# The chunk scan of an S5 layer: step innermost in the state tile, state copies in stages, and a new order of the phase behind it

## The chip, the core and the metric

The kernel runs on one core of a Trainium2 chip. The metric is the device time of one execution in microseconds, as the median of three runs. Matrix products run on TensorE, elementwise work on VectorE (DVE) and ScalarE (ACT), a few memsets on GpSimd (POOL); transfers are queued on SyncE (SP) and on ScalarE's queue. All arithmetic is float32; the large products are made of three products of rounded halves (`hi*hi + hi*lo + lo*hi`).

## What is computed

The model is an encoder of two layers over 512 tokens of width 1024. Layer 0 mixes tokens with a bidirectional diagonal state-space model (S5) and a GLU, layer 1 with a short gated convolution; each layer then attends to 256 memory tokens and applies a squared-ReLU MLP. The change lies in layer 0's mixer:

```python
u = (h @ w_in).reshape(bsz, seq, SSM_GROUPS, SSM_GROUP)      # 64 groups of 16
y = d * u
for r in range(2):                                           # two directions
    a_bar = exp(lam * dt)                                    # complex, 64 states a group
    bu = einsum('gph,lbgh->lbgp', b_bar, u)                  # flipped in time for r == 1
    states = associative_scan(a_r * a_l, a_r * b_l + b_r)    # x[l] = a_bar * x[l-1] + bu[l]
    y = y + einsum('ghp,lbgp->blgh', c, states).real         # flipped back for r == 1
z = gelu(y)
z = z * sigmoid(z @ w_glu)
return z @ w_out
```

## The kernel before

The 512 tokens are cut into 64 chunks of 8 (`NC = 64`, `T = 8`). Within a chunk the recurrence is unrolled into matrices; from chunk to chunk a complex state per group and state index is carried. The partitions hold both directions: 0 to 63 forward, 64 to 127 backward.

The stages around the change are these.

- `s_mats` (line 523): TensorE forms each chunk's contribution to the state, and ScalarE copies it from PSUM into `estate`, a tile of 128 partitions x [64 steps, 2 parts (real, imaginary), 64 groups].
- `scan_ops` (line 595): for step s = 1 to 63, VectorE makes four instructions of 128 elements each: two multiplies of the previous state by the powers `a1` and `a2` into scratch, and two adds into `estate[:, s]`. All are issued through the helper `tt` (line 312). `scan_run(n)` (line 776) runs the next n steps; for the first 12, VectorE also builds the tables `Q` in between.
- `strips` and `y_intra` (lines 544 and 579): TensorE builds the within-chunk matrices and applies them. Between them `kvp(n)` (line 712) advances the generator `kv0_gen` (line 630), which computes keys and values of the first cross-attention as a filler: eight blocks of 16 matmul steps. When a block ends, ScalarE evacuates it, and the next block but one is loaded by a DMA from ScalarE's queue.
- `p_part` (line 661) copies states from `estate` into `pt`, one tile for each eighth of the groups, shifted by one step, and reversed in time for the backward half. `p_early` copies the steps 0 to 41 of the blocks 0 to 3 within the scan, on ScalarE; `p_copy` the rest behind the scan, forward on VectorE and backward on ScalarE. The slot that has no predecessor is set to zero in each `pt` by GpSimd.
- `y_carry(i)` (line 587): TensorE adds the carried states' part of the output of a quarter of the groups. `y_evac` copies it out of PSUM (ScalarE and VectorE one half each), `z_rows` transposes it on TensorE, `z_gelu` applies the gelu on ScalarE and splits the result into halves on VectorE.
- `lin_block` (line 170) is one block of a large linear layer: 8 k-steps of six matmuls. Its weights come as 1 MB blocks through two staging buffers (`pump_dma`), and are split into halves by ScalarE (line 143) and VectorE (line 144) in `pump_split`. The first GLU block, `glu0`, takes the last quarter's `z_rows` and `z_gelu` in a hook.

Up to `glu0` the instructions of each engine run in the order in which they are written (`tc.manual_schedule()`); from `man.close()` on a planner sets the order, and it may place later work (the casts of keys and values, lines 1002 to 1006) ahead. Small tiles come from a pool of 30 pages (`NPG`); `estate` shares one large buffer with the tiles before and after it. The order behind the scan is:

```python
    y_intra(3)
    p_copy(0)
    p_copy(1)
    act.activation(warm, epsb, AF.Gelu_apprx_tanh)
    y_carry(0)
    for b in range(2, 6):
        p_copy(b)
    yt = y_evac(0)
    y_carry(1)
```

Of the kernel before, what the change touches and what calls it, by code (L numbers as in the profile page):

```python
# [19 lines left out]
P = 128  # L20
S = 512
D = 1024
KT = D // P
# [23 lines left out]
def tile_encoder(ctx, tc, xT, xN, memT, memN, small, b_re, b_im, c_re, c_im, a_w_in, a_w_glu,  # L47
# [23 lines left out]
    def page(shape, dt=F32, name="pg"):  # L71
        return pgpool.tile([P] + list(shape), dt, tag="pg", name=nm(name))

    def bank(shape, name="ps"):
        return pspool.tile([P] + list(shape), F32, tag="ps", name=nm(name))
# [54 lines left out]
    def pump_dma(ahead):  # L130
        while pos["dma"] < len(stream) and pos["dma"] - pos["split"] < ahead:
            loaded.append(stage_load(stream[pos["dma"]]))
            pos["dma"] += 1

    def pump_split(ahead):
        while pos["split"] < pos["dma"] and pos["split"] - pos["use"] < ahead:
            st = loaded[pos["split"]]
            tiles = []
            for half in range(2):
                src = st[:, 4 * half:4 * half + 4, :]  # L140
                hi = page([4, 256], F32R, "wh")
                lo = page([4, 256], F32R, "wl")
                act.copy(hi, src)  # L143
                v.tensor_tensor(out=lo, in0=src, in1=hi, op=ALU.subtract)  # L144
                tiles.append((hi, lo))
            split.append(tiles)
            pos["split"] += 1
# [22 lines left out]
    def lin_block(xs, hooks=None):  # L170

        t = next_block()
        ps = [bank([S], "lin") for _ in range(2)]
        for k in range(KT):
            if hooks and k in hooks:
                for f in hooks[k]:
                    f()
            xh, xl = xs(k)
            for m in range(2):
                mm3(ps[m], wsl(t, k, m, 0), wsl(t, k, m, 1), xh, xl, k == 0, k == KT - 1)  # L180
        return ps
# [25 lines left out]
    def split_to(a, k, src, from_act=True):  # L207
        if from_act:
            act.copy(a.hi(k), src)
        else:  # L210
            v.tensor_copy(a.hi(k), src)
        v.tensor_tensor(out=a.lo(k), in0=src, in1=a.hi(k), op=ALU.subtract)
# [246 lines left out]

    bb = s5pool.tile([P, 2, 65 * 16], F32, name="bb")  # L460
    nc.gpsimd.memset(bb[:, :, 64 * 16:], 0.0)
    estate = bpool.tile([P, NC, 2, G], F32, tag="big", name="estate")

    def gen_ops(b, X, xs, E, E2, flip, name):

# [42 lines left out]
    def sf_transpose(b):  # L508
        outp = []
        for ri in range(2):  # L510
            pg = page([8, P], F32, "sf")
            for hb in range(2):
                ps = bank([4, P], "tr")
                for i in range(4):
                    g = 4 * hb + i
                    pe.transpose(ps[:, i, :], sfT[b][ri][:, g].rearrange("p h j -> p (h j)"), ident)  # L516
                act.copy(pg[:, 4 * hb:4 * hb + 4, :], ps)
            outp.append(pg)
        sf[b] = outp
# [2 lines left out]

    def s_mats(b):
        for ri in range(2):
            ps = bank([NC, 8], "ps_s")
            for g in range(8):
                u = U[b // 2][:, 8 * (b % 2) + g, :]
                for r in range(2):
                    rs = slice(64 * r, 64 * r + 64)
                    pe.matmul(ps[rs, :, g], lhsT=sf[b][ri][:, g, rs], rhs=u[:, ::-1] if r else u,  # L530
                              start=True, stop=True)
            act.copy(estate[:, :, ri, 8 * b:8 * b + 8], ps)

    Q = {}

# [51 lines left out]
    def y_carry(i):  # L587
        for g in range(8):
            for ri in range(2):
                for b2 in range(2):  # L590
                    pe.matmul(yps[i][g // 4][64 * b2:64 * b2 + 64, g % 4, :], lhsT=pts[2 * i + b2][:, ri, g, :],
                              rhs=Q[2 * i + b2][ri][:, g].rearrange("p t h -> p (t h)"),
                              start=False, stop=(ri == 1 and g % 4 == 3))

    def scan_ops():
        for s in range(1, NC):
            xp = estate[:, s - 1]
            x = estate[:, s]
            t1_ = s5pool.tile([P, 2, G], F32, tag="sc1", name=nm("sc1"))
            t2_ = s5pool.tile([P, 2, G], F32, tag="sc2", name=nm("sc2"))  # L600
            yield (t1_, xp, a1, ALU.mult)
            yield (t2_, xp[:, ::-1, :], a2, ALU.mult)
            yield (x, x, t1_, ALU.add)
            yield (x, x, t2_, ALU.add)
# [51 lines left out]
                kv_load(i + 2)  # L656
            yield

    SE = 42

    def p_part(b, s0, s1, engs):

        for ri in range(2):
            e = estate[:, s0:s1, ri, 8 * b:8 * b + 8].rearrange("p s g -> p g s")
            engs[0](pts[b][0:64, ri, :, s0 + 1:s1 + 1], e[0:64])
            lo, hi = NC - 1 - s1, NC - 1 - s0
            engs[1](pts[b][64:128, ri, :, lo:hi], e[64:128, :, ::-1])  # L667

    def p_tile(b):
        pt = page([2, 8, NC], F32, "pt")  # L670
        nc.gpsimd.memset(pt[0:64, :, :, 0:1], 0.0)
        nc.gpsimd.memset(pt[64:128, :, :, NC - 1:NC], 0.0)
        pts[b] = pt

    def p_early(b):
        p_tile(b)
        p_part(b, 0, SE, (act.copy, act.copy))

    def p_copy(b):
        if b in pts:  # L680
            p_part(b, SE, NC - 1, (v.tensor_copy, act.copy))
        else:
            p_tile(b)
            p_part(b, 0, NC - 1, (v.tensor_copy, act.copy))


    ups = {}
# [24 lines left out]
    def kvp(n):  # L712
        for _ in range(n):
            next(kv_it, None)
# [34 lines left out]
    sf_transpose(2)  # L749
    sf_step(5)  # L750
    sf_transpose(3)
    s_mats(0)
    s_mats(1)
    mem_scale(mp, rm, 0)
# [21 lines left out]
    def scan_run(n, extra=()):  # L776

        extra = list(extra)
        for i in range(n):
            for j in range(4):  # L780
                tt(*sc[ns[0]])
                ns[0] += 1
                if j >= 2 and extra:
                    tt(*extra.pop(0))
        run_ops(extra)
# [17 lines left out]
    kvp(16)  # L803
    y_intra(2)
    scan_run(20)
    kvp(16)
    for b in range(4):
        p_early(b)
    kvp(48)
    scan_run(63 - 43)  # L810


    zf = []
# [2 lines left out]
    def y_evac(i):  # L816
        yt = page([T, 8, 16], F32, "yt")
        for q in range(2):
            o = yt[:, :, 4 * q:4 * q + 4, :]
            src = yps[i][q].rearrange("p g (t h) -> p t g h", t=T)  # L820
            if q == 0:
                act.copy(o, src)
            else:
                v.tensor_copy(o, src)
        return yt
# [3 lines left out]
    def z_rows(i, yt):  # L829
        zps[i] = [bank([4, P], "zT") for _ in range(2)]  # L830
        for q in range(2):
            for t in range(4):
                pe.transpose(zps[i][q][:, t, :], yt[:, 4 * q + t].rearrange("p g h -> p (g h)"), ident)
# [9 lines left out]
            tt(z.l[i][:, :, c], zf[i][:, :, c], z.h[i][:, :, c], ALU.subtract)  # L843

    y_intra(3)
    p_copy(0)
    p_copy(1)
    act.activation(warm, epsb, AF.Gelu_apprx_tanh)
    y_carry(0)
    for b in range(2, 6):  # L850
        p_copy(b)
    yt = y_evac(0)
    y_carry(1)
    p_copy(6)
    p_copy(7)
    for i in range(1, 4):
        z_rows(i - 1, yt)
        yt = y_evac(i)
        if i < 3:
            y_carry(i + 1)  # L860
        z_gelu(i - 1)
        if i == 2:
            pump_dma(2)
            pump_split(1)
    glu0 = lin_block(z, {2: [lambda: z_rows(3, yt), lambda: z_gelu(3)]})
    pump_dma(2)
    man.close()
    s5.close()

    tpool = ctx.enter_context(tc.tile_pool(name="tpool", bufs=8, reuse_waits="tile"))  # L870
# [14 lines left out]
    def norm_feed(k, st, a, vec):  # L885
# [3 lines left out]
            stt(a.lo(k), hk(k), gain(vec, k), a.hi(k), ALU.mult, ALU.subtract)  # L889
        st.add(hk(k), k == 0)  # L890


    z2 = Act2("z2")
    for i in range(4):
        ps = lin_block(z) if i else glu0
        pump()
        for m in range(2):
            k = 2 * i + m
            sg = tmp("sg")
            act.activation(sg, ps[m], AF.Sigmoid)  # L900
            tt(sg, sg, zf[i][:, m, :], ALU.mult)
            split_to(z2, k, sg)

    def residual_linear(xs, vec, hooks=None):
        a = Act2("hn")
# [9 lines left out]

    hnA, st = residual_linear(z2, G_XATT)


    def kv_tiles():
        kv = bpool.tile([P, 4, 2048], F32R, tag="big", name=nm("kv"))  # L920
        kh = [kv[:, i, :].rearrange("p (k n) -> p k n", k=KT) for i in range(2)]
        vh = [kv[:, 2 + i, :].rearrange("p (m n) -> p m n", m=2) for i in range(2)]
        return kh, vh

    def attention(hn_, st, kh, vh, vec):
        qa = Act2("q")
# [69 lines left out]
        transposes(2)  # L996
        hooks = {2: [lambda: o_block(2)], 3: [lambda: transposes(3)], 5: [lambda: o_block(3)]}
        return residual_linear(oa, vec, hooks)

    kh, vh = kv_tiles()  # L1000
    for i in range(2):
        act.copy(kh[0][:, 4 * i:4 * i + 4, :], K0[i])
        tt(kh[1][:, 4 * i:4 * i + 4, :], K0[i], kh[0][:, 4 * i:4 * i + 4, :], ALU.subtract)
        c = slice(512 * i, 512 * i + 512)
        act.copy(vh[0][:, :, c], V0[i])
        tt(vh[1][:, :, c], V0[i], vh[0][:, :, c], ALU.subtract)

    hnF, st = attention(hnA, st, kh, vh, G_FFN)

# [231 lines left out]
```

## Time and profile before

| what | value |
|---|---|
| median of three runs | 1475.1 us (1473.31 to 1475.87) |
| the profiled execution's own time | 1473.65 us |
| its span in the trace | 1471.9 us |
| granted TensorE clock, mean | 0.992 |
| busy: TensorE, VectorE, ScalarE | 97%, 59%, 36% |
| HBM read, written | 148.08 MB, 6.16 MB |

The page lists the busy time of each engine, the span in 40 slices, the DMA queues, the chain of work that ended last, and the costliest groups of instructions. TensorE's share is an average: it is full in the linear layers, and less so in the state-space phase, up to about 220 us. That phase is read from three views: a table of windows (busy time of each engine in a stretch), the timeline (instructions in order of time, with the idle time ahead of them and what ended it), and the instructions grouped by line and shape. A group's mean is the duration of one instruction; the next one can start a little before it ends.

### The profile page before, as it was taken

How to read it: one execution, taken by the hardware profiler on the slowest of the kernel's cores; microseconds unless marked ns; L12 is line 12 of the kernel's file. 1: busy time of each engine (PE TensorE's matmuls, PEld its weight loads, DVE VectorE, ACT ScalarE, POOL GpSimd, SP SyncE). 2: the span in 40 equal slices, each digit the busy share in tenths (PEclk: the TensorE clock that was granted, in tenths of full speed). 3: DMA queues.
4: the chain of work that ended last, by engine and by line, in shares of the span. 5: the costliest groups of instructions: out<-in, count | busy, mean ns of one | idle time of the engine just before them, and what ended most of it. 6: DMA issues, size and time to landing. Idle time of an engine off the chain costs nothing.

```text
span 1471.9 us, 19469 instructions
## 1 busy us (share of the span) xinstructions
PE 1432.1 (97%) x8146; PEld 1178.2 (80%) x8146; DVE 865.9 (59%) x1377; ACT 534.0 (36%) x799; POOL 4.9 (0%) x25
## 2 busy tenths in 40 slices
PE   8998879999999999999999999999999999999997
PEld 3586667888888888888888888988888888888886
DVE  8999966556565444444457546556666444544435
ACT  4661364434444132232333324433444323132221
POOL 0000000000000000000000000000000000000000
PEclk9999989999999999999999999999999999999999
DMA  8616515222133323323123224523024323323201
GB/s 291 199 50 177 151 56 200 86 86 87 58 114 115 115 86 93 107 86 109 63 73 128 86 87 143 193 77 103 30 86 143 114 86 91 110 86 110 90 1 58
DMA packets 157304, 155.50 MB, mean 106 GB/s; under 512 B 11424, under 2 KB 152864, under 8 KB 157216
## 3 DMA queue, kind: packets, MB, share of 16 engines
q1 hardware_dynamic: 149888, 146.91, 31.7%
q10 hardware_dynamic: 7328, 7.34, 1.6%
q8 instruction: 64, 1.05, 0.3%
q14 instruction: 24, 0.20, 0.0%
HBM read 148.08 MB, written 6.16 MB: 105 GB/s over the span
## 4 chain that ended last, share of the span: by engine, by line
PE 92%; DVE 4%; ACT 2%; DMA 1%; issue 0%; SPq 0%; ACTq 0%; DVEq 0%
PE lin L166 26%; PE lin L168 26%; PE lin L167 26%; PE u L693 4%; DVE estate L312 1%; DVE sc L312 1%; PE kv L168 1%; PE kv L167 1%; PE kv L166 1%; ACT pt L667 1%; PE ps_s L530 1%; PE tr L516 1%; PE kv L641 1%; PE kv L639 1%; DMA wd<-wt 1%; DVE Q L312 1%
## 5 line engine op out<-in xcount | busy, mean ns | idle before, releaser
L144 DVE TENSOR_TENSOR wl<-st,wh 128x1024 fp32r<-128x1024 f32 x224 | 270.6, 1222 | 171.5 <-ACT wh L143 170.9
L143 ACT CAST wh<-st 128x1024 fp32r<-128x1024 f32 x224 | 231.5, 1049 | 320.6 <-PE lin L167 292.2
L166 PE MATMUL lin<-hnh,wh 128*128 128x512 f32 x832 | 326.0, 392 | 0.0
L168 PE MATMUL lin<-hnh,wl 128*128 128x512 f32 x832 | 323.7, 389 | 0.0
L167 PE MATMUL lin<-hnl,wh 128*128 128x512 f32 x832 | 323.7, 389 | 0.0
L166 PE MATMUL lin<-mid,wh 128*128 128x512 f32 (+1 forms) x528 | 202.4, 383 | 0.0
L168 PE MATMUL lin<-mid,wl 128*128 128x512 f32 (+1 forms) x528 | 202.0, 383 | 0.0
L167 PE MATMUL lin<-mid,wh 128*128 128x512 f32 (+1 forms) x528 | 202.0, 383 | 0.0
L167 PEld LDWEIGHTS lin<-hnl,wh 128*128 128x128 f32 x832 | 156.2, 188 | 33.4 <-issue 1.2
L166 PEld LDWEIGHTS lin<-hnh,wh 128*128 128x128 f32 x832 | 156.2, 188 | 33.3 <-issue 1.2
L168 PEld LDWEIGHTS lin<-hnh,wl 128*128 128x128 f32 x832 | 156.2, 188 | 32.6
L168 PEld LDWEIGHTS lin<-mid,wl 128*128 128x128 f32 x528 | 99.2, 188 | 19.4
L166 PEld LDWEIGHTS lin<-mid,wh 128*128 128x128 f32 x528 | 99.2, 188 | 19.4
L167 PEld LDWEIGHTS lin<-mid,wh 128*128 128x128 f32 x528 | 99.2, 188 | 19.3
L312 DVE TENSOR_TENSOR relu<-relu,lin 128x512 f32<-128x512 f32 x64 | 43.7, 683 | 104.6 <-ACT relu L1025 104.6
L312 DVE TENSOR_TENSOR mo<-lin,r 128x512 f32<-128x512 f32 (+1 forms) x66 | 44.2, 675 | 102.1 <-PE lin L168 101.9
L1025 ACT ACTIVATE relu<-lin 128x512 f32<-128x512 f32 x64 | 38.0, 594 | 128.4 <-PE lin L168 128.0
L888 ACT ACTIVATE hnh<-h,sm 128x512 fp32r<-128x512 f32 x40 | 28.7, 718 | 132.0 <-DVE h L312 118.8
L693 PE MATMUL u<-xbig,st 128*128 128x512 f32 x128 | 58.4, 616 | 6.3 <-DMA st<-in_a_w_in_dram 6.3
L312 DVE TENSOR_TENSOR h<-lin,h 128x512 f32<-128x512 f32 x32 | 21.8, 692 | 67.3 <-PE lin L168 57.8
L1027 ACT CAST mid<-relu 128x512 fp32r<-128x512 f32 x64 | 39.6, 618 | 42.5 <-DVE relu L312 41.8
L693 PEld LDWEIGHTS u<-xbig,st 128*128 128x128 f32 x128 | 25.1, 198 | 37.2 <-issue 30.3
(214 smaller groups left out, 1934.9 us busy)
## 6 DMA issues: line engine op xcount, KB each, us to landing
st<-in_f_w_dram SPq DMA_DIRECT2D x64, 1024.0 KB, 5.7
st<-in_b_w_in_dram SPq DMA_DIRECT2D x12, 1024.0 KB, 5.1
st<-in_x_w_kv_dram SPq DMA_DIRECT2D x10, 1024.0 KB, 5.3
st<-in_x_w_q_dram SPq DMA_DIRECT2D x8, 1024.0 KB, 5.2
st<-in_x_w_o_dram SPq DMA_DIRECT2D x8, 1024.0 KB, 5.2
st<-in_x_w_kv_dram ACTq DMA_DIRECT2D x6, 1024.0 KB, 7.3
mt<-wd SPq DMA_DIRECT2D x32, 128.0 KB, 3.8
st<-in_a_w_glu_dram SPq DMA_DIRECT2D x4, 1024.0 KB, 5.6
```

The lines of the kernel that those rows point to most:

```text
L143: act.copy(hi, src)
L144: v.tensor_tensor(out=lo, in0=src, in1=hi, op=ALU.subtract)
L166: pe.matmul(ps, lhsT=wh, rhs=xh, start=start, stop=False)
L167: pe.matmul(ps, lhsT=wh, rhs=xl, start=False, stop=False)
L168: pe.matmul(ps, lhsT=wl, rhs=xh, start=False, stop=stop)
L312: v.tensor_tensor(out=o, in0=a, in1=b, op=op)
L516: pe.transpose(ps[:, i, :], sfT[b][ri][:, g].rearrange("p h j -> p (h j)"), ident)
L530: pe.matmul(ps[rs, :, g], lhsT=sf[b][ri][:, g, rs], rhs=u[:, ::-1] if r else u, start=True, stop=True)
L693: pe.matmul(ups[i, m], lhsT=win[i][:, k, m * P:(m + 1) * P], rhs=hn[k // 2][:, k % 2, :], start=(k == 0), stop=(k == KT - 1))
L888: act.activation(a.hi(k), hk(k), AF.Copy, scale=gain(vec, k))
L1025: act.activation(r_, ps[m], AF.Relu)
L1027: act.copy(md[:, k, 0, :], r_)
```

## The change

- `estate` becomes 128 partitions x [2 parts, 64 groups, 64 slots]: the step is now innermost. Slot 0 is set to zero once, and the contribution of chunk c goes to slot c + 1, so that slot s holds the state that chunk s needs. The last chunk's contribution isn't kept. The scan runs over s = 2 to 63, 62 steps.
- `s_mats` writes its PSUM tile in the order [group, chunk].
- `p_part` copies both parts in one instruction, without a shift; all eight blocks are copied in three stages: slots 0 to 35 behind step 43 in the written order, 36 to 51 behind step 51 (both halves on ScalarE), 52 to 63 behind the scan (VectorE and ScalarE). The memsets of the `pt` tiles go.
- `kvp(16)` and `kvp(48)` become `kvp(20)` and `kvp(32)`, with the first stage of the copies between them.
- The gelu table's load moves ahead of the last 11 steps; `pump_dma(2)` ahead of the last stage of copies.
- Behind the scan, `y_carry(i)` stands ahead of `z_rows(i - 1)`, two weight blocks are split in the loop, and the hook of `glu0` moves from k = 2 to k = 4.
- The casts of keys and values move into the GLU blocks 2 and 3, and `man.close()` behind those blocks: they run in the written order too.

```diff
-    estate = bpool.tile([P, NC, 2, G], F32, tag="big", name="estate")
+    estate = bpool.tile([P, 2, G, NC], F32, tag="big", name="estate")
...
-            ps = bank([NC, 8], "ps_s")
+            ps = bank([8, NC], "ps_s")
...
-                    pe.matmul(ps[rs, :, g], lhsT=sf[b][ri][:, g, rs], rhs=u[:, ::-1] if r else u,
+                    pe.matmul(ps[rs, g, :], lhsT=sf[b][ri][:, g, rs], rhs=u[:, ::-1] if r else u,
...
-            act.copy(estate[:, :, ri, 8 * b:8 * b + 8], ps)
+            act.copy(estate[:, ri, 8 * b:8 * b + 8, 1:NC], ps[:, :, 0:NC - 1])
...
-        for s in range(1, NC):
-            xp = estate[:, s - 1]
-            x = estate[:, s]
+        for s in range(2, NC):
+            xp = estate[:, :, :, s - 1]
+            x = estate[:, :, :, s]
...
     def p_part(b, s0, s1, engs):
-        for ri in range(2):
-            e = estate[:, s0:s1, ri, 8 * b:8 * b + 8].rearrange("p s g -> p g s")
-            engs[0](pts[b][0:64, ri, :, s0 + 1:s1 + 1], e[0:64])
-            lo, hi = NC - 1 - s1, NC - 1 - s0
-            engs[1](pts[b][64:128, ri, :, lo:hi], e[64:128, :, ::-1])
...
+        if b not in pts:
+            pts[b] = page([2, 8, NC], F32, "pt")
+        e = estate[:, :, 8 * b:8 * b + 8, s0:s1]
+        engs[0](pts[b][0:64, :, :, s0:s1], e[0:64])
+        engs[1](pts[b][64:128, :, :, NC - s1:NC - s0], e[64:128][:, :, :, ::-1])
...
+    nc.gpsimd.memset(estate[:, :, :, 0:1], 0.0)
     s_mats(0)
...
     scan_run(20)
-    kvp(16)
-    for b in range(4):
-        p_early(b)
-    kvp(48)
-    scan_run(63 - 43)
+    kvp(20)
+    for b in range(8):
+        p_part(b, 0, 36, (act.copy, act.copy))
+    kvp(32)
+    scan_run(8)
+    for b in range(8):
+        p_part(b, 36, 52, (act.copy, act.copy))
+    act.activation(warm, epsb, AF.Gelu_apprx_tanh)
+    scan_run(62 - 51)
...
     y_intra(3)
-    p_copy(0)
-    p_copy(1)
-    act.activation(warm, epsb, AF.Gelu_apprx_tanh)
+    pump_dma(2)
+    for b in range(8):
+        p_part(b, 52, NC, (v.tensor_copy, act.copy))
     y_carry(0)
-    for b in range(2, 6):
-        p_copy(b)
     yt = y_evac(0)
-    y_carry(1)
-    p_copy(6)
-    p_copy(7)
     for i in range(1, 4):
+        y_carry(i)
         z_rows(i - 1, yt)
+        if i < 3:
+            pump_split(i)
         yt = y_evac(i)
-        if i < 3:
-            y_carry(i + 1)
         z_gelu(i - 1)
-        if i == 2:
-            pump_dma(2)
-            pump_split(1)
-    glu0 = lin_block(z, {2: [lambda: z_rows(3, yt), lambda: z_gelu(3)]})
+    glu0 = lin_block(z, {4: [lambda: z_rows(3, yt), lambda: z_gelu(3)]})
     pump_dma(2)
-    man.close()
     s5.close()
...
+    def kv_cast(i):
+        act.copy(kh[0][:, 4 * i:4 * i + 4, :], K0[i])
+        tt(kh[1][:, 4 * i:4 * i + 4, :], K0[i], kh[0][:, 4 * i:4 * i + 4, :], ALU.subtract)
+        c = slice(512 * i, 512 * i + 512)
+        act.copy(vh[0][:, :, c], V0[i])
+        tt(vh[1][:, :, c], V0[i], vh[0][:, :, c], ALU.subtract)
...
     for i in range(4):
         ps = lin_block(z) if i else glu0
         pump()
...
+        if i >= 2:
+            kv_cast(i - 2)
+    man.close()
```

## Rows read from the trace of the kernel before

**Rows 1.** Page, first part: busy us, share of the span, instructions, by engine.
```profile
PE 1432.1 (97%) x8146; PEld 1178.2 (80%) x8146; DVE 865.9 (59%) x1377; ACT 534.0 (36%) x799; POOL 4.9 (0%) x25
```

**Rows 2.** Table of windows: stretch, its length, busy us by engine, clock, DMA.
```profile
109.00:172.00 63.00, 56.43 (x832) 45.32 (x831) 60.94 (x184) 5.97 (x11) 1.44 (x12) 0.95 0.66 175
205.00:221.50 16.50, 11.65 (x177) 10.65 (x174) 9.32 (x14) 15.50 (x21) 0.00 (x0) 1.00 0.00 1
233.00:280.00 47.00, 47.00 (x209) 38.93 (x208) 23.63 (x29) 19.56 (x28) 0.00 (x0) 1.00 0.45 149
```

**Rows 3.** Timeline: start, us, engine, line, operation; the scan's steps on VectorE.
```profile
143.05 0.49 DVE L312 TENSOR_TENSOR sc<-estate,a 128x128 f32<-128x128 f32 x2
...
144.10 0.49 DVE L312 TENSOR_TENSOR sc<-estate,a 128x128 f32<-128x128 f32 x2
...
195.18 0.61 DVE L312 TENSOR_TENSOR estate<-estate,sc 128x128 f32<-128x128 f32 x2
```

**Rows 4.** Timeline behind the scan: kv's last load, carries, transposes, first GLU matmuls.
```profile
182.11 0.37 ACTq L103 DMA_DIRECT2D st<-in_x_w_kv_dram  x1
...
187.48 7.89 PE L641 MATMUL kv<-st,mem 128*128 128x256 f32 x24 [9.53 <-DMA st<-in_x_w_kv_dram]
...
199.43 1.28 ACT L848 ACT_TABLE_LOAD   x1
...
207.19 1.09 PE L833 MATMUL zT<-sm,yt 128*128 128x128 f32 x8 [0.74 <-ACT yt L822]
208.21 3.71 PE L591 MATMUL y<-Q,pt 128*64 128x128 f32 x64
...
221.56 0.48 PE L166 MATMUL lin<-zsh,wh 128*128 128x512 f32 x1
...
223.91 0.50 PE L168 MATMUL lin<-zsh,wl 128*128 128x512 f32 x1 [1.64 <-DVE wl L144]
```

**Rows 5.** Groups by line and shape, VectorE, 0 to 260 us: count, busy us, mean ns.
```profile
L312 DVE TENSOR_TENSOR sc<-estate,a 128x128 f32<-128x128 f32 x126 | 31.0, 288 | 1.8
L312 DVE TENSOR_TENSOR zsl<-z,zsh 128x512 fp32r<-128x512 f32 x8 | 5.5, 690 | 0.2
L665 DVE COPY pt<-estate 64x504 f32<-64x504 f32 x8 | 4.3, 593 | 0.0
L842 DVE CAST zsh<-z 128x512 fp32r<-128x512 f32 x8 | 3.4, 421 | 0.0
L312 DVE TENSOR_TENSOR kv<-K,kv 128x1024 fp32r<-128x1024 f32 x2 | 2.4, 1222 | 7.1 <-ACT kv L1002 7.1
L665 DVE COPY pt<-estate 64x168 f32<-64x168 f32 x8 | 1.8, 288 | 0.0
L339 DVE CAST tab<-tab 128x64 int32<-128x64 f32 x2 | 0.4, 192 | 0.0
```

**Rows 6.** The same for ScalarE.
```profile
L667 ACT COPY pt<-estate 64x504 f32<-64x504 f32 x8 | 8.1, 1077 | 0.0
L209 ACT CAST z2h<-sg 128x512 fp32r<-128x512 f32 x6 | 3.7, 622 | 0.2
L667 ACT COPY pt<-estate 64x168 f32<-64x168 f32 x8 | 3.3, 484 | 0.0
L1002 ACT CAST kv<-K 128x1024 fp32r<-128x1024 f32 x2 | 2.1, 1042 | 0.0
```

**Rows 7.** Table of windows, TensorE only: length, busy us, granted clock, DMA.
```profile
191.50:192.50 1.00, 1.00 (x4) 0.50 0.00 0
192.50:193.50 1.00, 1.00 (x7) 1.00 0.00 0
```

**Rows 8.** Timeline: the two gelus of a quarter, and VectorE's first cast of them.
```profile
214.66 1.07 ACT L840 ACTIVATE z<-zT 128x512 f32<-128x512 f32 x2
...
215.76 0.42 DVE L842 CAST zsh<-z 128x512 fp32r<-128x512 f32 x1
```

More of the change, by code (lines that the diff above doesn't have):

```diff
@@ L657, in kv0_gen @@
             yield
-    SE = 42
     def p_part(b, s0, s1, engs):
-        for ri in range(2):
-            e = estate[:, s0:s1, ri, 8 * b:8 * b + 8].rearrange("p s g -> p g s")
-            engs[0](pts[b][0:64, ri, :, s0 + 1:s1 + 1], e[0:64])
-            lo, hi = NC - 1 - s1, NC - 1 - s0
-            engs[1](pts[b][64:128, ri, :, lo:hi], e[64:128, :, ::-1])
[L669 to L684, printed above, removed]
+        if b not in pts:
[3 more added lines that the diff above has]
+        engs[1](pts[b][64:128, :, :, NC - s1:NC - s0], e[64:128][:, :, :, ::-1])
     ups = {}
@@ L890, in norm_feed, with kv_tiles @@
         st.add(hk(k), k == 0)
+    def kv_tiles():
+        kv = bpool.tile([P, 4, 2048], F32R, tag="big", name=nm("kv"))
+        kh = [kv[:, i, :].rearrange("p (k n) -> p k n", k=KT) for i in range(2)]
+        vh = [kv[:, 2 + i, :].rearrange("p (m n) -> p m n", m=2) for i in range(2)]
+        return kh, vh
+    def kv_cast(i):
[4 more added lines that the diff above has]
+        tt(vh[1][:, :, c], V0[i], vh[0][:, :, c], ALU.subtract)
+    kh, vh = kv_tiles()
     z2 = Act2("z2")
@@ L916, in tile_encoder @@
     hnA, st = residual_linear(z2, G_XATT)
[L919 to L923, printed above, removed]
     def attention(hn_, st, kh, vh, vec):
@@ L998, in attention @@
         return residual_linear(oa, vec, hooks)
[L1000 to L1006, printed above, removed]
     hnF, st = attention(hnA, st, kh, vh, G_FFN)
```

## The prediction

> **What bounds the kernel now.** I read the page first: TensorE is busy 97% of the span [rows 1], so nearly all of the kernel is a stream of matmuls that this change doesn't touch. What it touches lies between about 75 and 280 us, so the table of windows comes next [rows 2]. From 109 to 172 us VectorE is busy for 61 of 63 us, and the scan is its work. From 205 to 221.5 us no engine but ScalarE is full (15.5 of 16.5 us), and TensorE stands for 5 us. In the GLU blocks, from 233 us on, TensorE is full, and VectorE and ScalarE are busy about half of the time: whatever moves there is covered.
>
> The timeline of VectorE gives the scan's pace: a step's first multiply starts at 143.05, the next one's at 144.10, 1.056 us for four instructions, with no idle time; the last two adds start at 195.18 and end at 195.79 [rows 3]. Call that moment E. Nothing that follows (state copies, carry matmuls, gelu, first GLU block) can finish before it. TensorE was late too: its last kv block waited 9.53 us for weights, whose DMA ScalarE's queue issued only at 182.11, behind copies, and ran on into the carry matmuls [rows 4]. So the end is set by E plus the tail: the first GLU matmul starts at 221.56, 25.8 us after E, and the second group waits another 1.64 us for its weights' low half [rows 4].
>
> **Part 1, the scan's layout.** Each step reads and writes `estate[:, :, :, s]`: 128 values per partition, 256 bytes apart. Before, they lay side by side. The count falls from 63 steps to 62 (-1.06 us), as the last state was never used. All four instructions of a step read a column; the two adds also write one. No row of before shows a two-input VectorE instruction on values that lie apart, so I bound it by the nearest rows.
> - Side by side, such an instruction takes 288 ns for 128 elements and 690 for 512: 1.047 ns per element and 154 fixed [rows 5].
> - VectorE copies: side by side 192 ns for 64 elements and 421 for 512, 0.51 ns each; out of the old estate, 512 bytes apart, 288 ns for 168 and 593 for 504, 0.91 ns each: 1.78 times [rows 5].
> - ScalarE: side by side 622 ns for 512 and 1042 for 1024, 0.82 ns each and 202 fixed; out of the old estate 484 ns for 168 and 1077 for 504, 1.765 ns each: 2.15 times [rows 6].
>
> Both engines pay for reading apart. Scaled by VectorE's ratio, an element of the scan takes 1.047 x 1.78 = 1.86 ns, 105 ns more per instruction. Other ways to carry the rows over: ScalarE's time per element as it stands, (1.765 - 1.047) x 128 = 92 ns; its ratio, (2.25 - 1.047) x 128 = 154 ns; and nothing, if only copies, which move two elements in the time of one, suffer. Below nothing is excluded: no row is faster apart. I take 105, from the same engine. 248 instructions x 105 ns = 26.0 us, all on the path, as VectorE has no idle time there. **E moves by 26.0 - 1.1 = +24.9 us** (bounds: +21.8 and +37.1; -1.1 for nothing).
>
> [...]
>
> The writes of the two adds are apart as well. No row shows such a write; I take them at nothing beyond the reads (they run alongside), with 238 ns per add as the other end (below, second rival).
>
> **Part 2, the state copies.** Before, copies of `estate` into `pt` ran in pieces: 16 on ScalarE inside the scan, 16 on VectorE and 16 on ScalarE behind it. Now both parts (real, imaginary) go in one instruction, runs of neighbours are read, and all eight blocks are copied in three stages. At ScalarE's rate for neighbours: 576 elements 0.67 us x 16 = 10.8 us, 256 elements 0.41 x 16 = 6.6 us, both under the scan steps that follow; if that cover were gone they would add up to 17 us (fourth rival). Behind the scan stay 8 copies of 192 elements on each engine, 0.36 us each, and the first carry needs two of them: about 0.9 us after E. The 16 POOL memsets and ScalarE's 1.28 us table load [rows 4] leave the tail.
>
> The kv pump moves too: `kvp(20)` ends a kv block, so the next weights' DMA is issued ahead of the copies on ScalarE's queue. The 9.53 us wait goes, but it buys nothing: the block that waited until 187.48 would start at about 178 and take 7.2 us, `y_intra(3)` 2 more, so TensorE is done by about 187 us, 33 us ahead of the new E, and stands. After the 9.53 us wait it ran at a granted clock of 0.50 for some 5 us before it had 1.00 [rows 7]; the first carry will pay that: half of 5 us, 2.5 us.
>
> **Part 3, the tail.** From E on TensorE does: 0.9 us wait, four carries of 3.71 us, three groups of transposes of 1.09 us [rows 4], 2.5 us for the clock: 0.9 + 14.8 + 3.3 + 2.5 = 21.5 us to the first GLU matmul, against 25.8. The order hides what ran between: `y_carry(i)` stands ahead of `z_rows(i-1)`, so an evacuation lies under a carry; two weight blocks are split under carries 1 and 2 (two casts of 1.04 us on ScalarE and two subtractions of 1.22 on VectorE each [rows 5, 6]), their DMAs having been issued on SP's queue as soon as kv frees the buffers, with nothing queued ahead of them. So the 1.64 us wait for `wl` goes as well. What is late next is the gelu of the last rows, now at k = 4 instead of 2: 12 matmuls (2.7 us, at 47 us for 209 [rows 2]) must hide transposes, gelu, cast and subtraction of the first half; I count 2.3 to 2.9 us and take it as hidden; bare, 1 us. **The tail gets shorter by 25.8 - 21.5 + 1.6 = 5.9 us.**
>
> **Part 4, the kv casts and the GLU blocks in written order.** Four ScalarE casts and four VectorE subtractions (1.04 and 1.22 us each [rows 5, 6]) leave the tail, where ScalarE was full, and go into GLU blocks 2 and 3: 2.1 us of ScalarE and 2.4 of VectorE per block of 10.8 us, on engines half idle there [rows 2]. K0 and V0 keep four of the 30 pages two blocks longer, so some `z2` and weight pages wait for half a block of TensorE; splits are a block ahead, so I cost it at nothing. Without that cover: 2 to 5 us, once.
>
> **Sum.** The profiled run took 1473.65 us, span 1471.9, 1.45 us under the median of the three runs, 1475.1. 1473.65 + 24.9 - 5.9 = **1492.6 us**, 1.3% slower. With the other two prices of a read: 1489.4 and 1504.8.
>
> **The rivals.**
> First, the scan keeps its pace (faster): a two-input instruction takes one element per 1.047 ns however far apart. For it: that is half the copies' rate, 0.51 ns, and the copies lost only down to 0.91 ns, still under 1.047 [rows 5]. Against it: ScalarE, which moves one element per 0.82 ns, drops to 1.765. Then 1473.65 - 1.1 - 5.9 = 1466.6 us. It decides below some 17 ns per instruction. [...]
> Second, writes apart cost as much as reads and come after them: another 1.86 ns x 128 x 124 adds = 29.5 us, 1522 us.
> Third, a small price of 17 to 40 ns, where tail and scan cancel: 1471 to 1476.5.
> Fourth, the change doesn't do what it says: as columns now interleave, the waits don't tell columns 0 to 36 from column 45, the copies don't run beside the scan, and the next steps wait for them: 10.8 + 6.6 us more, 1510 us. Against it: the second gelu wrote one half of the columns of `z` at once behind the first, before VectorE had read the other half, at 215.76 [rows 8].
>
> **How the numbers follow.** Forecast 0.66, first rival 0.17, second 0.07, third 0.05, fourth 0.05. The range must hold 8 in 10, so it reaches down to the first rival (1464 if the clock stays up) and up over the dearer read: 1464 to 1508; the likeliest case alone is 1487 to 1506. A measurement can tell about 0.2%, 3 us. Faster: 0.17; same: 0.05; slower: 0.66 + 0.07 + 0.05 = 0.78.
>
> **What would show it.** VectorE's scan rows, 288 ns before: near 393 the layout costs what I say; at 288 the first rival holds; adds at twice the multiplies' extra, the second. The pace per step should be 1.48 us and E near 220.7. VectorE idle between steps, behind ScalarE, is the fourth. First GLU matmul 21.5 us after E, no wait for `wl` in the first block, carry 0 at a clock of 0.50, no TensorE wait in GLU blocks 1 to 3. The forecast is wrong first of all if two inputs hide what one copy shows.

## The result

The changed kernel took 1491.9 us (median of four runs, 1490.23 to 1493.08) against 1474.7 for the one before (median of four as well): a ratio of 1.0115, with a 95% interval of 1.0103 to 1.0126. That is 1.15% slower; 1492.6 us had been forecast. The profiled execution's span grew from 1471.9 to 1490.3 us.

The groups by line and shape of the changed kernel (count, busy us, mean ns of one, idle time ahead of them), to be read beside [rows 5, 6]:

```profile
L312 DVE TENSOR_TENSOR estate<-estate,sc 128x128 f32<-128x128 f32 x124 | 51.6, 416 | 1.7
L312 DVE TENSOR_TENSOR sc<-estate,a 128x128 f32<-128x128 f32 x124 | 40.5, 368 | 1.8
L665 DVE COPY pt<-estate 64x192 f32<-64x192 f32 x8 | 1.4, 246 | 0.0
...
L665 ACT COPY pt<-estate 64x576 f32<-64x576 f32 x8 | 5.4, 672 | 9.5 <-DVE estate L312 9.4
L665 ACT COPY pt<-estate 64x256 f32<-64x256 f32 x8 | 3.2, 404 | 11.5 <-DVE estate L312 11.4
L666 ACT COPY pt<-estate 64x192 f32<-64x192 f32 x8 | 2.1, 342 | 9.3 <-DVE estate L312 9.3
```

The same group of adds in the kernel before:

```profile
L312 DVE TENSOR_TENSOR estate<-estate,sc 128x128 f32<-128x128 f32 x126 | 36.2, 288 | 1.8
```

The multiplies went from 288 [rows 5] to 368 ns, the adds from 288 to 416. The scan's 248 instructions thus cost 124 x 80 + 124 x 128 ns = 25.8 us more. ScalarE's copies became cheap, 672 ns for 576 elements, where before 504 took 1077.

The timeline of the changed kernel at the scan's end (start, us, engine, line, operation, idle time ahead):

```profile
109.99 0.66 DVE L312 TENSOR_TENSOR sc<-estate,a 128x128 f32<-128x128 f32 x2
...
219.91 0.64 DVE L312 TENSOR_TENSOR sc<-estate,a 128x128 f32<-128x128 f32 x2
220.47 0.85 DVE L312 TENSOR_TENSOR estate<-estate,sc 128x128 f32<-128x128 f32 x2
...
221.76 10.06 PE L592 MATMUL y<-Q,pt 128*64 128x128 f32 x128 [26.00 <-ACT pt L666]
...
241.94 0.47 PE L166 MATMUL lin<-zsh,wh 128*128 128x512 f32 x1
```

The scan ends at 221.3 us instead of 195.8. From there to the first GLU matmul it is 20.6 us instead of 25.8, and the 1.64 us wait behind it [rows 4] is gone. 25.5 - 5.2 - 1.6 = 18.7 us is the growth of the span to within 0.3.

And the windows of the changed kernel (stretch, length, busy us of PE, PEld, DVE, ACT, POOL, granted clock, DMA):

```profile
180.00:221.30 41.30, 8.72 (x56) 7.38 (x54) 39.38 (x113) 19.73 (x36) 0.00 (x0) 0.62 0.15 48
221.30:242.00 20.70, 20.24 (x281) 19.40 (x281) 12.88 (x25) 10.71 (x21) 0.00 (x0) 0.85 0.33 103
254.00:298.00 44.00, 44.00 (x195) 36.44 (x195) 25.65 (x30) 20.60 (x28) 0.00 (x0) 1.00 0.34 109
```

Ahead of the scan's end VectorE works 39.4 of 41.3 us and TensorE 8.7; behind it TensorE is the full engine, where before it stood for 5 of 16.5 us [rows 2]. The GLU blocks show no wait of TensorE.

In the kernel before, TensorE's waits behind the scan's end were these, besides the 0.74 us of [rows 4]:

```profile
198.83 7.62 PE L591 MATMUL y<-Q,pt 128*64 128x128 f32 x128
...
214.86 1.06 PE L833 MATMUL zT<-sm,yt 128*128 128x128 f32 x8 [2.94 <-ACT kv L1002]
...
220.74 1.07 PE L833 MATMUL zT<-sm,yt 128*128 128x128 f32 x8 [1.17 <-DVE yt L824]
```

It came to the first carry 3.0 us after the scan's end, as its own last kv block was late [rows 4], and then waited 0.74, 2.94 and 1.17 us: 7.9 us in all. The changed kernel has 0.4 us of this left, and pays 2.4 us more for its first two carries (10.06 against 7.62 us); that makes the 5.2 us.

### The profile page after: what moved, and what is told of

Read it like the earlier page. It is cut to its first block, busy times and chain, and to the rows that moved or that the text cites. A ratio compares the mean times of both kernels' runs of the same rounds, so it can differ in the third digit from the quotient of the medians.

```text
span 1490.3 us, 19448 instructions
## 1 busy us (share of the span) xinstructions
PE 1433.3 (96%) x8146; PEld 1180.8 (79%) x8146; DVE 886.8 (60%) x1365; ACT 529.8 (36%) x807; POOL 1.0 (0%) x10
## 4 chain that ended last, share of the span: by engine, by line
PE 84%; DVE 9%; issue 0%; ACT 0%; DVEq 0%
PE lin L166 25%; PE lin L168 25%; PE lin L167 25%; DVE estate L312 3%; DVE sc L312 3%; DVE Q L312 2%; PE y L592 1%; PE kv L168 1%; PE kv L167 1%; PE kv L166 1%; DVE gt L312 1%; PE sc L168 1%; PE sc L167 1%; PE sc L166 1%; PE o L166 0%; PE o L167 0%
```

## The experiments

Two questions were open. Is it really the operands' distance that slows the scan, and how does its price come about? And is it the new order that shortened the tail? The theory was: the price is the distance's, and the order gains the tail. The rivals: the scan is slowed by something beside it (ScalarE reading the same tile), and the tail got shorter for another reason.

**The price of a distance, by itself.** The kernel before, with groups of 12 instructions of 128 elements put in behind the state copies, on scratch:

```diff
+        pbig = bpool.tile([P, 8192], F32, tag="big", name="probe")
...
+        def col(st, i):
+            return pbig[:, i:i + 127 * st + 1:st]
...
+        for _ in range(12): tt(po, pa, pb_, ALU.add)
+        for _ in range(12): tt(po, col(2, 0), pa, ALU.add)
...
+        for _ in range(12): tt(po, col(64, 0), col(64, 1), ALU.add)
...
+        for _ in range(12): tt(col(64, 0), col(64, 0), pa, ALU.add)
...
```

> The kernel before, with groups of 12 VectorE and ScalarE instructions of 128 elements put in behind the state copies; they only fill scratch, and the run's time is not used. Operands lie side by side, or 8, 16, 32 or 256 bytes apart, as first input, as second input, as both, as output, and as input and output at once. Theory (what counts is the reads and writes that lie apart): side by side near 288 ns, one input 256 bytes apart near 368 (the scan's multiply of the changed kernel), input and output apart near 416 (its add). [...] Rival (the scan slowed for another reason, such as ScalarE reading the same tile): 288 for all. Open: what an output apart costs alone; 48 ns more if it only adds to a read, 80 or more if a write is priced like a read.

Groups by line in short windows of that run, one row each for: side by side; first input 8, 16 and 256 bytes apart; second input 256 apart; both inputs; output 8, 16 and 256 apart; input and output 8, 16 and 256 apart. The number ahead of the last bar is the mean in ns.

```profile
L312 DVE TENSOR_TENSOR po<-pa,pb 128x128 f32<-128x128 f32 x5 | 1.5, 293 | 0.2
...
L312 DVE TENSOR_TENSOR po<-probe,pa 128x128 f32<-128x128 f32 x5 | 1.5, 293 | 0.2
L312 DVE TENSOR_TENSOR po<-probe,pa 128x128 f32<-128x128 f32 x4 | 1.5, 378 | 0.1
L312 DVE TENSOR_TENSOR po<-probe,pa 128x128 f32<-128x128 f32 x4 | 1.5, 366 | 0.1
L312 DVE TENSOR_TENSOR po<-pa,probe 128x128 f32<-128x128 f32 x4 | 1.5, 376 | 0.1
L312 DVE TENSOR_TENSOR po<-probe 128x128 f32<-128x128 f32 x4 | 1.8, 442 | 0.1
...
L312 DVE TENSOR_TENSOR probe<-pa,pb 128x128 f32<-128x128 f32 x4 | 1.2, 293 | 0.1
L312 DVE TENSOR_TENSOR probe<-pa,pb 128x128 f32<-128x128 f32 x4 | 1.5, 385 | 0.1
L312 DVE TENSOR_TENSOR probe<-pa,pb 128x128 f32<-128x128 f32 x4 | 1.5, 374 | 0.1
...
L312 DVE TENSOR_TENSOR probe<-probe,pa 128x128 f32<-128x128 f32 x5 | 1.5, 293 | 0.2
L312 DVE TENSOR_TENSOR probe<-probe,pa 128x128 f32<-128x128 f32 x4 | 1.5, 384 | 0.1
L312 DVE TENSOR_TENSOR probe<-probe,pa 128x128 f32<-128x128 f32 x4 | 1.7, 416 | 0.1
```

And copies in the same run, by line (min/median/max ns): VectorE side by side, reading and writing 256 bytes apart; ScalarE reading 8, 16 and 256 bytes apart, side by side, and writing 256 bytes apart.

```profile
L885 DVE COPY po<-pa x12: 220/227/228, 298.9 to 301.8; 128x128 f32<-128x128 f32 x12
L886 DVE COPY po<-probe x12: 299/299/303, 302.1 to 305.8; 128x128 f32<-128x128 f32 x12
L887 DVE COPY probe<-pa x12: 307/308/309, 306.1 to 309.9; 128x128 f32<-128x128 f32 x12
L888 ACT COPY po<-probe x12: 302/303/305, 310.2 to 313.9; 128x128 f32<-128x128 f32 x12
L889 ACT COPY po<-probe x12: 415/415/415, 314.2 to 319.1; 128x128 f32<-128x128 f32 x12
L890 ACT COPY po<-probe x12: 404/405/406, 319.6 to 324.4; 128x128 f32<-128x128 f32 x12
L891 ACT COPY po<-pa x12: 297/298/298, 324.8 to 328.4; 128x128 f32<-128x128 f32 x12
L892 ACT COPY probe<-pa x12: 398/403/405, 328.6 to 333.4; 128x128 f32<-128x128 f32 x12
```

The scan's two prices are reproduced while ScalarE stands (for 96.9 us, until its first copy at 310.2): 366 ns for a read, 416 for a read and a write 256 bytes apart. In the changed kernel itself, from 196 to 203.8 us, no engine but VectorE is busy, and the adds still take 410 ns and the multiplies 363. So no neighbour engine is needed, and that rival falls. A distance of 8 bytes was free or nearly so wherever it was tried (293 ns, as side by side; 303 against 298 on ScalarE), and for a single operand 16 bytes cost as much as 256 or a little more (378 and 366 ns for a read, 385 and 374 for a write): there is a step, not a slope. A write alone cost about as much as a read (374 against 366); together they cost 123 ns, less than the sum of 73 and 81.

**The layout alone.** The kernel before with the step innermost, 63 steps, the old copies and order:

```diff
-    estate = bpool.tile([P, NC, 2, G], F32, tag="big", name="estate")
+    estate = bpool.tile([P, 2, G, NC], F32, tag="big", name="estate")
...
-            xp = estate[:, s - 1]
-            x = estate[:, s]
+            xp = estate[:, :, :, s - 1]
+            x = estate[:, :, :, s]
...
```

> The kernel before with the new layout alone: step innermost, 63 steps, no empty slot, copies and order as before. Theory: 63 steps x 4 x 104 ns = 26.2 us more scan; ScalarE's copies behind the scan read neighbours and give back 3 to 4 us; the carry pays 1 to 2.5 us for a low clock: 1496 to 1500 us. Rival (the scan's slow steps belong to the staged copies beside it): 1471 to 1476 us.

It took 1492.9 us, a ratio of 1.0127 (1.0111 to 1.0142): within the scatter, all that the whole change does. The interesting rows are those of the tail, in the timeline of that run:

```profile
220.91 0.87 DVE L312 TENSOR_TENSOR estate<-estate,sc 128x128 f32<-128x128 f32 x2
...
222.07 9.40 PE L591 MATMUL y<-Q,pt 128*64 128x128 f32 x128 [9.68 <-DVE pt L665]
...
241.58 0.48 PE L166 MATMUL lin<-zsh,wh 128*128 128x512 f32 x1
```

From the scan's end (221.8) to the first GLU matmul it is 19.8 us, in the old order, with the kv casts in the tail. So the new order isn't needed for the shorter tail. What shortens it, this run alone can't say: ScalarE's copies are cheap in it, but the scan is slow in it too, and TensorE comes to the first carry in time (0.3 us after the scan's end, 3.0 before). The pair layout below, with the fast scan, separates the two. The expectation of 3 to 4 us for the copies was too small, and with it the 1496 to 1500 us.

**All but the layout.** The changed kernel, with the step outermost again:

```diff
-    estate = bpool.tile([P, 2, G, NC], F32, tag="big", name="estate")
+    estate = bpool.tile([P, NC, 2, G], F32, tag="big", name="estate")
...
-        e = estate[:, :, 8 * b:8 * b + 8, s0:s1]
+        e = estate[:, s0:s1, :, 8 * b:8 * b + 8].rearrange("p s r g -> p r g s")
...
```

> The changed kernel with the old layout (step outermost), keeping the empty first slot, 62 steps, the staged copies, the order behind the scan and the kv casts in the GLU blocks. Theory: the scan is back at 288 ns, it ends near 194.7 us, and the tail is about 20.6 us; ScalarE's copies read apart again (1.2 us for 576 elements, 0.64 for 256) and finish 1 to 2 us behind the scan, so 1466 to 1469 us. Rival (the tail got shorter only because the slow scan gave ScalarE and TensorE time to finish first): the tail is back near 25 us and the time near 1473 us.

It took 1475.2 us, a ratio of 1.0005 (0.9996 to 1.0013) to the kernel before. My expectation failed, and the rival came nearer: the slow scan had been ScalarE's cover, as the timeline shows:

```profile
191.69 1.19 ACT L666 COPY pt<-estate 64x576 f32<-64x576 f32 x1
...
195.65 2.34 DVE L665 COPY pt<-estate 64x192 f32<-64x192 f32 x8
...
204.14 1.28 ACT L796 ACT_TABLE_LOAD   x1
...
206.24 9.10 PE L592 MATMUL y<-Q,pt 128*64 128x128 f32 x128 [9.02 <-ACT pt L666]
...
225.45 0.47 PE L166 MATMUL lin<-zsh,wh 128*128 128x512 f32 x1
```

The scan is back at 288 ns and ends at 195.6. But ScalarE, reading apart, needs 1.2 us per copy, is done with the first stage at 192.9 and with the second at 204.1. The carry can't start before 206.2, which eats what the scan saves. I had expected ScalarE 1 to 2 us behind the scan; it was 10, since its first copy began at 173.5, behind the evacuation of a kv block, and not when slot 35 was ready.

**The same, with ScalarE's copies begun earlier.** If ScalarE alone holds that tail, its copies have to start where it is idle:

```diff
     y_intra(2)
+    for b in range(8):
+        p_part(b, 0, 22, (act.copy, act.copy))
     scan_run(20)
...
-        p_part(b, 0, 36, (act.copy, act.copy))
+        p_part(b, 22, 44, (act.copy, act.copy))
...
-        p_part(b, 36, 52, (act.copy, act.copy))
+        p_part(b, 44, 52, (act.copy, act.copy))
```

> The changed kernel with the old layout (step outermost, as in the run with the tail alone), but the first stage of copies split: slots 0 to 21 behind y_intra(2), where ScalarE is idle, then 22 to 43, 44 to 51, and 52 to 63 as before. Theory (with the old layout the tail was long only because ScalarE's slow copies ran on for 10 us behind the scan): ScalarE is done with the stages about 1 to 2 us behind the scan, first carry near 198 us instead of 206.2, 1467 to 1470 us. Rival (something else in the new order holds the tail): no change, 1475 us.

1467.7 us, a ratio of 0.9953 (0.9940 to 0.9966). The first carry starts at 197.85 instead of 206.24, the first GLU matmul stands at 216.78, 20.9 us behind the scan's end. So copies that read apart hold the tail only where they begin too late.

**A layout for both.** From the probe a third layout follows: pairs of steps innermost. The scan's operands then lie 8 bytes apart, and a copy reads two neighbours at a time. Once in the changed kernel:

```diff
-    estate = bpool.tile([P, 2, G, NC], F32, tag="big", name="estate")
+    estate = bpool.tile([P, NC // 2, 2, G, 2], F32, tag="big", name="estate")
...
-            xp = estate[:, :, :, s - 1]
-            x = estate[:, :, :, s]
+            xp = estate[:, (s - 1) // 2, :, :, (s - 1) % 2]
+            x = estate[:, s // 2, :, :, s % 2]
...
-        e = estate[:, :, 8 * b:8 * b + 8, s0:s1]
+        e = estate[:, s0 // 2:s1 // 2, :, 8 * b:8 * b + 8, :].rearrange("p s r g t -> p r g s t")
...
```

> The changed kernel with a third layout: the tile holds pairs of steps innermost (step pair, part, group, step within the pair), so that the scan's operands lie 8 bytes apart and the state copies still read two neighbours at a time; ScalarE evacuates s_mats in two copies of even and odd slots. All else as in the changed kernel. Theory (the scan pays only from 16 bytes apart, the tail got shorter because the copies read neighbours): scan instructions back at 285 to 293 ns, its end near 195.7 us, copies of 576 elements near 0.67 us, first GLU matmul 20 to 21 us later, 1466 to 1469 us. Rival (the layout's price is not the distance of 16 bytes but any step off the neighbour): scan at 368 and 416 ns and 1490 us or more. Rival (pairs are too short for ScalarE): copies of 576 elements near 1.2 us and the first carry some 10 us behind the scan, about 1475 us.

and once in the kernel before, with its order, the same tile lines, 62 steps, the empty slot and both parts in one copy:

> The kernel before with the pair layout, the empty first slot and 62 steps; copies, kv pump, kv casts and the order behind the scan as before, but each copy takes both parts. Theory (the shorter tail comes from the cheap copies, and the new order is worth about 1 us): scan end near 195.7 us, first GLU matmul about 20 us later, 1467 to 1470 us, within 2 us of the run with the new order. Rival (as the prediction had it, the new order shortens the tail by some 6 us): 1472 to 1475 us.

They took 1466.8 and 1466.9 us, a ratio of 0.9947 (0.9935 to 0.9960) each: faster than both kernels. Groups by line of the one with the new order:

```profile
L312 DVE TENSOR_TENSOR estate<-estate,sc 128x128 f32<-128x128 f32 x124 | 35.8, 289 | 1.7
L312 DVE TENSOR_TENSOR sc<-estate,a 128x128 f32<-128x128 f32 x124 | 30.6, 288 | 1.8
...
L668 ACT COPY pt<-estate 64x576 f32<-64x576 f32 x8 | 5.7, 709 | 0.1
L668 ACT COPY pt<-estate 64x256 f32<-64x256 f32 x8 | 3.3, 418 | 0.1
L669 ACT COPY pt<-estate 64x192 f32<-64x192 f32 x8 | 2.2, 351 | 2.3 <-DVE estate L312 2.3
```

and the timeline of the one with the old order:

```profile
181.65 7.15 PE L642 MATMUL kv<-st,mem 128*128 128x256 f32 x32 [1.39 <-DMA st<-in_x_w_kv_dram]
...
195.32 0.61 DVE L312 TENSOR_TENSOR estate<-estate,sc 128x128 f32<-128x128 f32 x2
...
196.51 9.42 PE L592 MATMUL y<-Q,pt 128*64 128x128 f32 x128 [5.82 <-ACT pt L667]
...
216.05 0.48 PE L166 MATMUL lin<-zsh,wh 128*128 128x512 f32 x1
```

The scan is back at 288 ns, copies cost 709 instead of 672 ns. In the old order the first GLU matmul stands 20.1 us behind the scan's end, and the time is the same as in the new order. The scan is fast here, so it is the cheaper copies that shorten the tail, and with them no gain of the new order can be measured. (They are cheaper by reading neighbours and by being fewer, both parts at once; the two weren't taken apart.) TensorE's last kv block also starts earlier, at 181.65 instead of 187.48, as the DMA of its weights is issued at 175.98 instead of 182.11 [rows 4], among the copies; so TensorE is done with it before the scan ends.

**The clock.** The changed kernel, with 27 matmuls into an unused bank, so that TensorE works until the scan's end:

```diff
+    wp = fbank([S], "warmps")
+    for _ in range(27):
+        pe.matmul(wp, lhsT=ones, rhs=Q[0][0][:, 0:4].rearrange("p a t h -> p (a t h)"), start=True, stop=True)
     y_intra(3)
```

> The changed kernel with 27 float32 matmuls of 512 columns into an unused PSUM bank ahead of y_intra(3), so that TensorE works until the scan's end; nothing reads them. Theory (the first carries pay for a clock at 0.50): the two carries take 7.6 us instead of 10.1, time lower by about 2.4 us, near 1489.5. Rival (something else sets the pace there, such as the evacuations): no change, 1491.9.

1490.6 us, a ratio of 1.0110 (1.0096 to 1.0123); 1.3 us under the changed kernel and too near to its 1.0115 to be told from it. So it ran once more beside the changed kernel, and once in the pair layout with 9 matmuls:

> The changed kernel itself, on the chip of the next two runs, so that the price of the low clock is read in one job: 1490 to 1493 us.

> The changed kernel with the 27 unread matmuls ahead of y_intra(3), as before, now beside the changed kernel. Theory (the carries' low clock costs what the carries lose, 2.6 us): 2.0 to 2.8 us under the changed kernel. Rival (part of it is given back, since the first run was only about 1.3 us under it): 1 to 1.6 us under it.

> The pair layout with the new order, and 9 unread matmuls between the last kv block and y_intra(3), so that TensorE doesn't stand for the 10 us ahead of the carries. Theory (the low clock costs about 2 us in this kernel too): the first two carries near 7.5 us, 1464 to 1465.5 us. Rival: no change, 1466.8 us.

They took 1491.4, 1491.3 and 1466.1 us, with ratios of 1.0112 (1.0098 to 1.0126), 1.0111 (1.0095 to 1.0126) and 0.9942 (0.9929 to 0.9954). None of the three expected gains shows clearly in the times: the second run with the extra matmuls is 0.1 us under the changed kernel beside it, less than even the rival's 1 us, and the pair layout came out 0.7 us lower, which can't be told from no change. The local effect is as expected. The first two rows are windows of the changed kernel (length, TensorE's busy us, granted clock, DMA): its carries start at a granted clock of 0.50 and have 1.00 only some 6 us later. The rows behind them are the timeline of the second run with the extra matmuls:

```profile
225.70:226.70 1.00, 1.00 (x12) 0.50 0.00 0
227.70:228.70 1.00, 1.00 (x23) 1.00 0.06 16
```

```profile
222.94 7.45 PE L592 MATMUL y<-Q,pt 128*64 128x128 f32 x128 [2.26 <-ACT pt L666]
...
240.50 0.48 PE L166 MATMUL lin<-zsh,wh 128*128 128x512 f32 x1
```

The two carries take 7.45 us instead of 10.06 (9.65 in the second execution of the changed kernel), and from the first carry to the first GLU matmul it is 17.6 us instead of 20.2 (19.8). Somewhat less than half a microsecond went back into the scan: between 206 and 218 us an add took 417 ns and a multiply 370 while TensorE worked, 411 and 364 while it stood; over TensorE's pause of 26 us, some 17 steps, that makes 17 x 4 x 6 ns = 0.4 us. From the scan's first multiply to the first GLU matmul the profiled executions with the extra matmuls take 129.75 and 129.69 us, those without 131.95 and 131.57: some 2 us are gained there. Behind it they lose 0.5 us again in both pairs, all of it in the last 50 us of the kernel, for a reason that wasn't looked for. The rest can't be settled: the scan's start alone differed by 2.1 us between the two profiled executions (108.73 and 110.81).

## Why the prediction was right, and where it wasn't

The forecast of 1492.6 us lies 0.7 us off the median. It was right for the reason that decided it, but two terms of the sum were right only as sums, and that is luck.

- **The price of the scan.** 26.0 us forecast, 25.8 measured. A read apart was taken at 105 ns; it cost 80. The writes of the adds were taken at nothing; they cost 48 more. The step that failed is "they run alongside". The two errors cancel, by luck: 105 against a mean of 104. The carried-over time per element of ScalarE (92 ns) was nearer to a read than VectorE's ratio (105). The rows that the prediction calls copies side by side are casts [rows 5]; the probe's plain copy of 128 elements, 227 ns, lies on their line, so nothing hung on it.
- **The scan's end.** From the first step to the last it took 86.7 us before and 111.3 after: 24.6 us more, 24.9 forecast.
- **The copies.** 0.67, 0.40 and 0.34 us measured, 0.67, 0.41 and 0.36 forecast, under the scan, as forecast. The first carry started 0.4 us behind the scan, not 0.9. One queue was overlooked: `y_intra(3)` ended at 195.8 and not at 187, as its banks waited 7.04 us for ScalarE to evacuate the last kv blocks behind the first stage of copies. It cost nothing, as TensorE had time.
- **The tail.** 5.9 us forecast, 6.8 measured (5.2 and 1.6). The size holds, the reason doesn't. The prediction put it down to the new order ("The order hides what ran between"). The layout alone has it too (19.8 us to the first GLU matmul), the order with the old layout doesn't have it (29.8 us), and in the pair layout both orders take the same time. What had held the tail was ScalarE, full in [rows 2] with copies that read apart. The prediction had seen ScalarE full and had priced the cheaper copies, but it counted them only inside the scan and for the wait ahead of the first carry, and gave what TensorE had waited behind it to the order.
- **The clock.** 2.5 us forecast, 2.4 measured on the two carries (10.06 against 7.62 us); its worth in the total stays open, as above.
- **The GLU blocks and the kv casts.** Forecast at nothing; TensorE had no wait there.
- **The rivals.** The first, that the scan keeps its pace, fell: 368 and 416 ns, and with it the third (17 to 40 ns more). The second, that writes cost on top, held in kind, at 48 ns for an add and not 238. The fourth fell: ScalarE's first stage ran from 180.5 to 191.4 us while VectorE went on.

## What to carry to other kernels

A layout has several readers: price each of them per element, on its own engine, and multiply by how often it runs on the path. Here a chain of 62 dependent steps, 248 instructions, paid for 48 copies. If two users want different neighbours, look for a layout that gives each of them just enough; with float32, pairs were enough for both engines (the scan's instructions at 288 and 289 ns, ScalarE's copies of 576 elements at 709 instead of 672). And a full engine in a stage is the one to relieve. Here the new order gained nothing while ScalarE's copies read apart and began late (1475.2 us), and nothing measurable once they were cheap; what helped was to make them cheaper (1466.9 us in the old order) or to begin them earlier (1467.7).

## What the runs showed of the hardware that was not expected

- The price of a distance came as a step. A two-input VectorE instruction on 128 float32 elements took 293 ns with its first input 4 or 8 bytes apart, 378 at 16, 380 at 32 and 366 at 256. ScalarE's copy of 128 elements took 298, 303, 415 and 405 ns when it read 4, 8, 16 and 256 bytes apart.
- Writes cost about what reads do: 385, 388 and 374 ns with the output 16, 32 and 256 bytes apart. Two operands apart cost less than the sum of their prices: two reads at 256 bytes 442 ns, a read and a write 416, and at 16 bytes only 384, no more than the write alone.
- From 206 to 218 us an instruction of the scan took some 4 to 7 ns longer in the two runs in which TensorE worked there (adds 416 and 417 ns, multiplies 368 and 370) than in the two in which it stood (411 and 410, 364 and 363). The reason wasn't followed further.
